# A hybrid decoder layer on one core: which weights are split by an accumulating transfer, and where the first casts and transposes stand

## The chip, the core and the metric

One core of a Trainium2 chip runs the whole layer as one program. TensorE (PE) multiplies, VectorE (DVE), ScalarE (ACT) and GpSimd (POOL) do elementwise work, SyncE (SP) issues transfers, and POOL issues some too. Each engine works through its own instructions in a fixed order. The metric is the device time of one execution in microseconds (us); less is better.

## The reference

One decoder layer in float32 with 1024 tokens of width 1024, cut to what matters here:

```
xn   = rms_norm(x, norm_mix)
proj = xn @ w_in          # [q | k/v for three branches | gates | conv in | q_mem | 3 merge gates]
...
a, ag = split(conv_in);  u = a * sigmoid(ag)      # then a causal convolution of 31 taps
...
qm = rms_norm(q_mem, mem_qk_norm[0])              # 4 heads of 128
km, vm = split(rms_norm(mem, norm_mem) @ w_mem_kv)
o_m = softmax(qm @ km.T) @ vm
...
merged = gm[0]*br_nsa + gm[1]*br_conv + gm[2]*br_mem
h = x + merged @ w_out
out = h + (silu(rms_norm(h) @ w_gate) * (rms_norm(h) @ w_up)) @ w_down
```

## The kernel before

Products are taken in float32r, a rounded form of float32 that TensorE runs in one pass. To keep the precision every operand is split in two tiles, high = rounded value and low = value - high, and a product is three matmuls: high x high, high x low, low x high (`mm3`, L151). For data the split (`split`, L130) is a cast on ACT and a subtraction on DVE. For most weights it is done otherwise (`unit`, L246, lines 254 to 257): ACT casts the loaded tile to the high half, ACT writes the negative of that into the low half, and a transfer that POOL issues adds the loaded tile to it in place. The loaded tile ("st", two buffers, or "fst", one buffer, for fill) can be loaded anew only when the transfer has landed; the split weights ("wsl") have three buffers, those for fill ("fsl") two.

The stages in the order of the program:

- Start: four pairs of row tiles of x (256 rows each). For each pair `norm_pair` (L200) takes two row sums of squares and roots on ACT, scales the rows on DVE (L207), transposes them on TensorE (16 transposes, L216) and splits the result into the eight tiles XN. `raw_proj` (L319) multiplies a pair with the first weights, the queries of the memory attention, heads 0 and 1 (48 products of 256 columns). The loop at L337 normalises and transposes pair tp + 1 ahead of the products of pair tp.
- The convolution's gate and input (L374 to L384, products of 512 columns), and from then on DVE's 124 taps (L371), laid along the products of the later stages.
- The branch gates, the inputs of the compressed keys and values (L410, whose sums are on POOL), their small network.
- The memory's norm and its keys and values (L480 to L492): eight weight tiles in four pairs.
- Memory attention for two pairs of heads (L552), which takes the next query products along; head norms (`head_norms`, L303).
- Convolution's layer norm, keys and values of two branches, attention, then the merge and the feed-forward part, which the change leaves alone.
- Fill (L781 to L794): the products for the merge gates, 24 weight tiles of 48 products of 512 columns, at the lowest priority. They go into the one PSUM bank named "pf"; after 24 products ACT copies it to "fz" (L793) and the bank is free again. Twelve of the tiles may run any time, the others are spread over the attention.

The order of each engine's instructions is fixed when the program is built, by a list scheduler that follows priorities (program order, with fill and taps put behind), its own estimate of durations, and order-only dependencies that the program adds by hand (`tc.add_manual_dep` with `ORDER`). At run time an instruction waits for its data and for the instruction before it on its engine.

Of the kernel before, what the change touches and what calls it, by code (L numbers as in the profile page):

```python
# [39 lines left out]
def hybrid_layer_kernel(  # L40
# [86 lines left out]
    def sub(eng, o, a, b):  # L127
        eng.tensor_tensor(o, a, b, op=OP.subtract)  # L128

    def split(hi, lo, src, eng=None):  # L130
        nc.scalar.copy(hi, src)  # L131
        sub(eng or nc.vector, lo, src, hi.bitcast(F32))

    def recip_rms(ss, n, eps, w):
        r = small(w)
        nc.scalar.activation(r, ss, AF.Sqrt, scale=1.0 / n, bias=eps)
        q = small(w)
        nc.vector.reciprocal(q, r)
        return q

    products = []

# [56 lines left out]

    def norm_pair(src, gain, dests, js):  # L200

        for tt in range(2):
            j = js[tt]
            ss = small(1)
            nc.scalar.activation(j, src[:, tt, :], AF.Square, accum_out=ss)
            r = recip_rms(ss, D, RMS_EPS, 1)
            nc.vector.scalar_tensor_tensor(j, src[:, tt, :], r, gain, op0=OP.mult, op1=OP.mult)  # L207
        transpose_pair(js, dests)

    def transpose_pair(js, dests):  # L210
        for kp in range(4):
            b = bank([2, 256])
            for kk in range(2):
                k = 2 * kp + kk
                for tt in range(2):
                    nc.tensor.transpose(b[:, kk, tt * P:(tt + 1) * P], js[tt][:, k * P:(k + 1) * P], ident)  # L216
            hi, lo = dests(kp)
            split(hi, lo, b)
# [16 lines left out]

    def norm_x(tp):
        half, q = tp // 2, tp % 2
        js = work2()
        if q == 0:
            for kp in range(4):  # L240
                XN[half][kp] = slab([2, 2, 512])
        norm_pair(xin[tp], gmix, lambda kp: tuple(XN[half][kp][:, hl, :, q * 256:(q + 1) * 256] for hl in range(2)),
                  js)


    def unit(src, shape, alloc=wslab, eng=None, load=False):  # L246
        if alloc is fslab:
            st = fstp.tile([P] + shape, F32, tag="fst", name=nm("fst"))
        else:
            st = stage.tile([P] + shape, F32, tag="st", name=nm("st"))  # L250
        ld = nc.sync.dma_start(st, src)
        w = alloc([2] + shape)
        hi, lo = w[:, 0], w[:, 1]
        if alloc is fslab or alloc is wslab:
            nc.scalar.copy(hi, st)
# [9 lines left out]

    def row_units(w, c0, alloc=wslab, eng=None):
        return [unit(w[u * 512:(u + 1) * 512, c0:c0 + 256].rearrange("(k p) c -> p k c", p=P), [4, 256], alloc, eng)
                for u in range(2)]

# [58 lines left out]
    for half in range(2):  # L328
        b = bank([512])
        nc.tensor.matmul(b, ones[0:1, :], g1[half], start=True, stop=True)  # L330
        nc.scalar.activation(gmix[:, half * 512:(half + 1) * 512], b, AF.Copy, scale=512.0)
    ws = row_units(w_in, C_QM)
    xin += [rows2(x, tp * 256) for tp in range(1, 4)]
    nc.sync.dma_start(gm, mem_qk_norm.to_broadcast([P, 2, P]))
    norm_x(0)
    QMQ = {}
    for tp in range(4):  # L337
        if tp < 3:
            norm_x(tp + 1)
        if tp == 0:  # L340
            QMQ[0] = slab([NT, 2, P], F32)
        raw_proj(ws, tp, QMQ[0])
# [31 lines left out]
    for ct in range(4):  # L374
        wag = col_unit(w_in, C_AG + ct * P)
        wa = col_unit(w_in, C_A + ct * P)
        uc = slab([2, S], F32)
# [32 lines left out]
    def compress_in(kind, c0):  # L410
        w = col_unit(w_in, c0, eng=nc.gpsimd)
        raw = t4([2, 512])
# [77 lines left out]
    for hp in range(2):  # L490
        ps = tok_proj(row_units(w_mem_kv, 512 + hp * 256, eng=nc.gpsimd), 0, mn)
        split(VM[:, 0, :, hp * 256:(hp + 1) * 256], VM[:, 1, :, hp * 256:(hp + 1) * 256], ps)  # L492
# [70 lines left out]

    QMQ[1] = slab([NT, 2, P], F32)
    mem_attention(0, row_units(w_in, C_QM + 256, eng=nc.gpsimd), QMQ[1])
    head_norms(QMQ[1], gm[:, 0, :])
    Q = [slab([NT, 4, 64], F32) for _ in range(2)]
    mem_attention(1, row_units(w_in, C_Q, eng=nc.gpsimd), Q[0])
    head_norms(Q[0], None)


    ws = row_units(w_in, C_Q + 256, eng=nc.gpsimd)
    for tp in range(4):
# [46 lines left out]
    for s, K, V in ((0, KS, VS), (1, KW, VW)):  # L620
        ws = row_units(w_in, C_KV + s * 256, eng=nc.gpsimd)

# [555 lines left out]
```

## Time and profile before

| | |
|---|---|
| median of the 3 runs shown | 1756.53 us (1756.08 to 1757.57) |
| the profiled execution | 1755.66 us, its span 1754.0 us |
| TensorE busy | 1710.8 us, 98% of the span |
| DVE, ACT, POOL busy | 58%, 45%, 33% |
| mean granted TensorE clock | 0.993 |
| accumulating transfers | 30 into "wsl", 24 into "fsl", 512 KB each |

In rows of the timeline the first number is the start, the second the time of the row's instructions together, then engine, line, operation, output <- input, sizes, and xN for N instructions; in brackets stands the idle time before them and what ended it. In rows of waits: the engine and its tile, what it waited for, microseconds in total, how often, the longest. A busy TensorE is not a TensorE at full rate, since the granted clock is lower for some time after idling.

### The profile page before, as it was taken

How to read it: one execution, taken by the hardware profiler on the slowest of the kernel's cores; microseconds unless marked ns; L12 is line 12 of the kernel's file. 1: busy time of each engine (PE TensorE's matmuls, PEld its weight loads, DVE VectorE, ACT ScalarE, POOL GpSimd, SP SyncE). 2: the span in 40 equal slices, each digit the busy share in tenths (PEclk: the TensorE clock that was granted, in tenths of full speed). 3: DMA queues.
4: the chain of work that ended last, by engine and by line, in shares of the span. 5: the costliest groups of instructions: out<-in, count | busy, mean ns of one | idle time of the engine just before them, and what ended most of it. 6: DMA issues, size and time to landing. Idle time of an engine off the chain costs nothing. (4 is left out here: it accounts for less than half of the span.)

```text
span 1754.0 us, 25341 instructions
## 1 busy us (share of the span) xinstructions
PE 1710.8 (98%) x9483; PEld 1488.0 (85%) x9483; DVE 1014.3 (58%) x1725; ACT 785.6 (45%) x1434; POOL 578.5 (33%) x549
## 2 busy tenths in 40 slices
PE   6899989999999999999999999999999999999999
PEld 5787879899988889999888899788888888888887
DVE  2488967635434556667754532865555454457655
ACT  5422554445366666767654422642222233233332
POOL 1100523224134434334303510156556767410000
PEclk9999999999999999999999999999999999999999
DMA  8344674544134222212286322233333445794673
GB/s 237 81 87 109 178 171 109 131 103 120 37 100 112 76 79 61 58 43 73 77 286 219 126 79 82 93 103 115 96 106 111 145 149 170 245 397 155 221 237 124
DMA packets 186165, 232.41 MB, mean 133 GB/s; under 512 B 11638, under 2 KB 126614, under 8 KB 185018
## 3 DMA queue, kind: packets, MB, share of 16 engines
q1 hardware_dynamic: 178266, 202.47, 34.8%
q0 software_dynamic: 7776, 28.32, 8.7%
q8 instruction: 75, 1.23, 0.3%
q14 instruction: 48, 0.39, 0.1%
HBM read 152.10 MB, written 50.33 MB: 115 GB/s over the span
## 5 line engine op out<-in xcount | busy, mean ns | idle before, releaser
L144 PE MATMUL ps<-slab,wsl 128*128 128x512 f32 (+1 forms) x1664 | 373.6, 383 | 6.1 <-POOL slab L423 3.1
L144 PEld LDWEIGHTS ps<-slab,wsl 128*128 128x128 f32 x1664 | 304.8, 190 | 67.2 <-POOL slab L423 3.3
L144 PE MATMUL pf<-slab,fsl 128*128 128x512 f32 x1236 | 322.4, 400 | 7.9 <-ACT fz L793 5.0
L144 PEld LDWEIGHTS pf<-slab,fsl 128*128 128x128 f32 x1236 | 224.4, 189 | 49.5 <-ACT fz L793 6.1
L144 PE MATMUL ps<-wsl,slab 128*128 128x256 f32 x1680 | 222.5, 289 | 6.7 <-DMA wsl<-st 5.7
L144 PEld LDWEIGHTS ps<-wsl,slab 128*128 128x128 f32 x1680 | 213.7, 197 | 10.1 <-DMA wsl<-st 6.6
L371 DVE SCALAR_TENSOR_TENSOR slab<-slab,cw 128x1021 f32<-128x1021 f32 (+15 forms) x120 | 163.1, 1362 | 2.4
L1008 DVE TENSOR_TENSOR t<-ps,t 128x512 f32<-128x512 f32 x127 | 86.9, 688 | 115.3 <-PE ps L144 114.1
L144 PE MATMUL ps<-slab,fsl 128*128 128x512 f32 x636 | 147.7, 389 | 0.0
L144 PEld LDWEIGHTS ps<-slab,fsl 128*128 128x128 f32 x636 | 119.4, 188 | 24.8
L128 DVE TENSOR_TENSOR t<-ps,t 128x512 fp32r<-128x512 f32 (+3 forms) x196 | 120.5, 632 | 31.5 <-ACT t L131 30.4
L1112 PE MATMUL ps<-wsl 128*128 128x512 f32 x495 | 118.5, 389 | 0.0
L144 PE MATMUL ps<-t,slab 128*128 128x256 f32 x624 | 116.3, 292 | 0.8 <-DVE t L128 0.8
L131 ACT CAST t<-ps 128x512 fp32r<-128x512 f32 (+2 forms) x192 | 98.9, 541 | 38.5 <-PE ps L742 26.6
L1112 PEld LDWEIGHTS ps<-wsl 128*128 128x128 f32 x495 | 92.9, 188 | 19.3
L144 PEld LDWEIGHTS ps<-t,slab 128*128 128x128 f32 x624 | 94.2, 190 | 6.6 <-DVE t L128 1.2
L144 PE MATMUL ps<-slab,qt 128*128 128x384 f32 (+3 forms) x384 | 95.1, 340 | 0.0
L656 POOL TENSOR_SCALAR wsl<-wsl,sm,gsb 128x640 f32<-128x640 f32 (+7 forms) x76 | 58.6, 781 | 93.1 <-DVE sm L651 86.6
L131 ACT CAST wsl<-t 128x1024 fp32r<-128x1024 f32 x42 | 44.3, 1054 | 98.3 <-POOL t L128 35.1
L257 POOL DMA_DIRECT2D wsl<-st x30 | 26.2, 883 | 182.4 <-ACT wsl L256 140.7
L1112 PE MATMUL ps<-fsl 128*128 128x512 f32 x330 | 79.8, 389 | 0.0
L1021 POOL TENSOR_TENSOR t<-t,t 128x512 f32<-128x512 f32 x21 | 39.2, 1865 | 116.7 <-DVE t L1008 43.8
(235 smaller groups left out, 2807.3 us busy)
## 6 DMA issues: line engine op xcount, KB each, us to landing
t<-in_w_down_dram SPq DMA_DIRECT2D x70, 256.0 KB, 4.3
wsl<-st POOLq DMA_DIRECT2D x30, 512.0 KB, 5.2
fst<-in_w_in_dram SPq DMA_DIRECT2D x24, 512.0 KB, 3.9
fsl<-fst POOLq DMA_DIRECT2D x24, 512.0 KB, 4.5
zd<-fz SPq DMA_DIRECT2D x48, 256.0 KB, 2.1
t<-zd SPq DMA_DIRECT2D x24, 512.0 KB, 3.9
st<-in_w_in_dram SPq DMA_DIRECT2D x22, 512.0 KB, 5.3
st<-in_w_gate_dram SPq DMA_DIRECT2D x22, 512.0 KB, 4.0
```

Source lines behind the costliest of these rows:

```text
L128: eng.tensor_tensor(o, a, b, op=OP.subtract)
L131: nc.scalar.copy(hi, src)
L144: m = nc.tensor.matmul(o, a, b, start=start, stop=stop)
L257: nc.gpsimd.dma_start(lo, st, accum_op=OP.add)
L371: return nc.vector.scalar_tensor_tensor(acc[:, s:], u[:, :S - s], cw[:, ct, 30 - s:31 - s], acc[:, s:], op0=OP.mult, op1=OP.add)
L656: nc.gpsimd.tensor_scalar(tiles[h], tiles[h], rec[:, h:h + 1], gsb[:, i, c0:c0 + 1], op0=OP.mult, op1=OP.mult)
L1008: nc.vector.tensor_tensor(o, a_, b_, op=OP.add)
L1021: nc.gpsimd.tensor_tensor(u4, u4, c22, op=OP.mult)
L1112: nc.tensor.matmul(B[t], a_, b_, start=start and k == 0 and j == 0, stop=k == FH - 1 and j == 2, skip_group_check=True)
```

## The change

`split` takes an engine as before, and with `nc.sync` it now does the negation and the accumulating transfer; without an engine DVE subtracts, with `nc.gpsimd` POOL does. `unit` no longer decides by the buffer, but by the engine that its caller names. The callers are set so: the convolution's weights, the compressed branches' inputs, the later query weights, the keys' and values' weights and fill from its fourth tile on keep the transfer (`eng=nc.sync`); the first weights and the eight tiles of the memory's keys and values go to DVE; the first three fill tiles go to POOL.

The casts of the first weights (`ready`) are taken out of the load and put, by an order-only dependency, behind the last root of pair 0 (`roots[-1]`). `norm_x` and the transposes (`turn_x`) are separate now: the transposes of pair 1 get an order-only dependency on the last product of pair 0, and those of the later pairs stand behind the products of the pair before in program order.

```
     def split(hi, lo, src, eng=None):
-        nc.scalar.copy(hi, src)
-        sub(eng or nc.vector, lo, src, hi.bitcast(F32))
+        first = nc.scalar.copy(hi, src)
+        if eng is nc.sync:
+            nc.scalar.activation(lo, hi.bitcast(F32), AF.Copy, scale=-1.0)
+            nc.gpsimd.dma_start(lo, src, accum_op=OP.add)
+        else:
+            sub(eng or nc.vector, lo, src, hi.bitcast(F32))
+        return first.ins
...
     def recip_rms(ss, n, eps, w):
         r = small(w)
-        nc.scalar.activation(r, ss, AF.Sqrt, scale=1.0 / n, bias=eps)
+        roots.append(nc.scalar.activation(r, ss, AF.Sqrt, scale=1.0 / n, bias=eps).ins)
...
-    def transpose_pair(js, dests):
+    def transpose_pair(js, dests, after=None):
...
-                    nc.tensor.transpose(b[:, kk, tt * P:(tt + 1) * P], js[tt][:, k * P:(k + 1) * P], ident)
+                    m = nc.tensor.transpose(b[:, kk, tt * P:(tt + 1) * P], js[tt][:, k * P:(k + 1) * P], ident)
+                    if after is not None:
+                        tc.add_manual_dep(m.ins, after.name, ORDER, reason="behind the products of the tiles before")
...
     def norm_x(tp):
+        js = work2()
+        norm_rows(xin[tp], gmix, js)
+        return js
+
+    def turn_x(tp, js, after=None):
         half, q = tp // 2, tp % 2
...
-        hi, lo = w[:, 0], w[:, 1]
-        if alloc is fslab or alloc is wslab:
-            nc.scalar.copy(hi, st)
-            nc.scalar.activation(lo, hi.bitcast(F32), AF.Copy, scale=-1.0)
-            nc.gpsimd.dma_start(lo, st, accum_op=OP.add)
+        if eng is None and ready is not None:
+            ready.append((w, st))
         else:
-            split(hi, lo, st, eng)
+            split(w[:, 0], w[:, 1], st, eng)
...
-    ws = row_units(w_in, C_QM)
+    ready = []
+    ws = row_units(w_in, C_QM, ready=ready)
...
-    norm_x(0)
-    QMQ = {}
+    turn_x(0, norm_x(0))
+    for w, st in ready:
+        tc.add_manual_dep(split(w[:, 0], w[:, 1], st), roots[-1].name, ORDER, reason="behind the first rows' sums")
+    js = norm_x(1)
+    QMQ = {0: slab([NT, 2, P], F32)}
     for tp in range(4):
-        if tp < 3:
-            norm_x(tp + 1)
-        if tp == 0:
-            QMQ[0] = slab([NT, 2, P], F32)
+        if tp:
+            turn_x(tp, js, products[-1][0] if tp == 1 else None)
+            js = norm_x(tp + 1) if tp < 3 else None
         raw_proj(ws, tp, QMQ[0])
...
-        wag = col_unit(w_in, C_AG + ct * P)
+        wag = col_unit(w_in, C_AG + ct * P, eng=nc.sync)
...
-        ps = tok_proj(row_units(w_mem_kv, hp * 256, eng=nc.gpsimd), 0, mn).rearrange("p t (h d) -> p t h d", h=2)
+        ps = tok_proj(row_units(w_mem_kv, hp * 256), 0, mn).rearrange("p t (h d) -> p t h d", h=2)
...
-            w = col_unit(w_in, C_GM + b_ * D + d_ * P, alloc=fslab, eng=nc.gpsimd)
+            w = col_unit(w_in, C_GM + b_ * D + d_ * P, alloc=fslab, eng=nc.sync if n_ > 2 else nc.gpsimd)
```

What this does to the order. On TensorE at the start, before, from the end of pair 0's transposes on (slab_175 holds pair 0's scaled rows, slab_222 pair 1's, slab_176 and slab_177 are tiles of XN, wsl_155 is the first weight tile):

```order
L216 MATMUL ps_215<-ident,slab_175 128x128 x3
L216 MATMUL ps_237<-ident,slab_222 128x128
L216 MATMUL ps_244<-ident,slab_222 128x128
L216 MATMUL ps_251<-ident,slab_222 128x128
L216 MATMUL ps_258<-ident,slab_222 128x128
L144 MATMUL ps_266<-wsl_155,slab_176 128x256
L216 MATMUL ps_237<-ident,slab_222 128x128 x3
L216 MATMUL ps_244<-ident,slab_222 128x128 x3
L216 MATMUL ps_251<-ident,slab_222 128x128 x3
L216 MATMUL ps_258<-ident,slab_222 128x128 x3
L144 MATMUL ps_266<-wsl_155,slab_176 128x256 x5
L144 MATMUL ps_266<-wsl_155,slab_177 128x256 x6
```

The same place now (slab_169 is pair 0, slab_220 pair 1, slab_184 to slab_187 tiles of XN, wsl_155 and wsl_158 the two weight tiles):

```order
L223 MATMUL ps_209<-ident,slab_169 128x128 x3
L149 MATMUL ps_236<-wsl_155,slab_184 128x256 x6
L149 MATMUL ps_236<-wsl_155,slab_185 128x256 x6
L149 MATMUL ps_236<-wsl_158,slab_186 128x256 x6
L149 MATMUL ps_236<-wsl_158,slab_187 128x256 x6
L149 MATMUL ps_236<-wsl_155,slab_184 128x256 x6
L149 MATMUL ps_236<-wsl_155,slab_185 128x256 x6
L149 MATMUL ps_236<-wsl_158,slab_186 128x256 x6
L149 MATMUL ps_236<-wsl_158,slab_187 128x256 x6
L223 MATMUL ps_286<-ident,slab_220 128x128
L223 MATMUL ps_293<-ident,slab_220 128x128
```

All 48 products of pair 0 stand ahead of pair 1's transposes now; before, one did. Further on, the second and third pair's products are no longer one block, and the first gate products of the convolution stand between pair 3's.

On ACT at the start, before, from the first row sum of pair 0 on (slab_143 is pair 0 as loaded, st_153 and st_159 are the loaded weights):

```order
L205 ACTIVATE slab_175,sm_180<-slab_143 128x1024
L136 ACTIVATE sm_182<-sm_180 128x1
L255 CAST wsl_155<-st_153 128x1024
L205 ACTIVATE slab_175,sm_187<-slab_143 128x1024
L256 ACTIVATE wsl_155<-wsl_155 128x1024
L255 CAST wsl_161<-st_159 128x1024
L136 ACTIVATE sm_189<-sm_187 128x1
L256 ACTIVATE wsl_161<-wsl_161 128x1024
L131 CAST slab_176<-ps_194 128x2x256
```

And now:

```order
L209 ACTIVATE slab_169,sm_170<-slab_143 128x1024
L141 ACTIVATE sm_172<-sm_170 128x1
L209 ACTIVATE slab_169,sm_177<-slab_143 128x1024
L141 ACTIVATE sm_179<-sm_177 128x1
L131 CAST wsl_155<-st_153 128x1024
L131 CAST wsl_158<-st_156 128x1024
L131 CAST slab_184<-ps_188 128x2x256
```

Both sums and roots of pair 0 stand ahead of the weights' casts, and the two negations are gone.

On DVE in the stage of the memory's keys and values, before (slab_850 is the third quarter of the convolution, the narrow numbers are its taps' lengths, t_188 the squares of the first pair's keys):

```order
L371 SCALAR_TENSOR_TENSOR slab_850<-slab_850,cw 128x1008
L293 TENSOR_REDUCE sm_1498<-t_188_1496 128x4
L128 TENSOR_TENSOR t_220_1736<-ps_1731,t_220_1736 128x512
L138 RECIPROCAL sm_1502<-sm_1500 128x4
L296 TENSOR_TENSOR t_187_1495<-ps_1446,sm_1502 128x512
L371 SCALAR_TENSOR_TENSOR slab_850<-slab_850,cw 128x1007
```

And now (wsl_1516, wsl_1588 and wsl_1593 are the weight tiles u3, u4 and u5 of eight):

```order
L383 SCALAR_TENSOR_TENSOR slab_848<-slab_848,cw 128x1008
L128 TENSOR_TENSOR wsl_1516<-st_1514,wsl_1516 128x1024
L302 TENSOR_REDUCE sm_1494<-t_188_1492 128x4
L383 SCALAR_TENSOR_TENSOR slab_848<-slab_848,cw 128x1007
L128 TENSOR_TENSOR wsl_1588<-st_1586,wsl_1588 128x1024
L128 TENSOR_TENSOR t_220_1726<-ps_1721,t_220_1726 128x512
L143 RECIPROCAL sm_1498<-sm_1496 128x4
L383 SCALAR_TENSOR_TENSOR slab_848<-slab_848,cw 128x1006
L305 TENSOR_TENSOR t_187_1491<-ps_1442,sm_1498 128x512
L383 SCALAR_TENSOR_TENSOR slab_848<-slab_848,cw 128x1005
L128 TENSOR_TENSOR wsl_1593<-st_1591,wsl_1593 128x1024
```

The weights' subtractions stand among the taps and the key norms. Later on TensorE, the order of fill among the other products is new too; until the first scores of the attention 408 fill products stand there now, before 360.

More of the change, by code (lines that the diff above doesn't have):

```diff
@@ L139, in recip_rms @@
         return q
-    products = []
+    products, roots = [], []
     def mm(o, a, b, start, stop):
@@ L198, in gain_row, with norm_rows @@
         return g
-    def norm_pair(src, gain, dests, js):
+    def norm_rows(src, gain, js):
         for tt in range(2):
@@ L207, in norm_pair @@
             nc.vector.scalar_tensor_tensor(j, src[:, tt, :], r, gain, op0=OP.mult, op1=OP.mult)
+    def norm_pair(src, gain, dests, js):
+        norm_rows(src, gain, js)
         transpose_pair(js, dests)
-    def transpose_pair(js, dests):
+    def transpose_pair(js, dests, after=None):
         for kp in range(4):
@@ L236, in norm_x @@
     def norm_x(tp):
+        js = work2()
+        norm_rows(xin[tp], gmix, js)
+        return js
+    def turn_x(tp, js, after=None):
         half, q = tp // 2, tp % 2
-        js = work2()
         if q == 0:
@@ L241, in norm_x, with unit @@
                 XN[half][kp] = slab([2, 2, 512])
-        norm_pair(xin[tp], gmix, lambda kp: tuple(XN[half][kp][:, hl, :, q * 256:(q + 1) * 256] for hl in range(2)),
-                  js)
-    def unit(src, shape, alloc=wslab, eng=None, load=False):
+        transpose_pair(js, lambda kp: tuple(XN[half][kp][:, hl, :, q * 256:(q + 1) * 256] for hl in range(2)), after)
+    def unit(src, shape, alloc=wslab, eng=None, load=False, ready=None):
         if alloc is fslab:
@@ L264, in col_unit, with row_units @@
                     load)
-    def row_units(w, c0, alloc=wslab, eng=None):
-        return [unit(w[u * 512:(u + 1) * 512, c0:c0 + 256].rearrange("(k p) c -> p k c", p=P), [4, 256], alloc, eng)
-                for u in range(2)]
+    def row_units(w, c0, alloc=wslab, eng=None, ready=None):
+        return [unit(w[u * 512:(u + 1) * 512, c0:c0 + 256].rearrange("(k p) c -> p k c", p=P), [4, 256], alloc, eng,
+                     ready=ready) for u in range(2)]
     def chan_proj(w, half, act=xn, n=P, alloc=bank):
@@ L374, in hybrid_layer_kernel @@
     for ct in range(4):
-        wag = col_unit(w_in, C_AG + ct * P)
-        wa = col_unit(w_in, C_A + ct * P)
+        wag = col_unit(w_in, C_AG + ct * P, eng=nc.sync)
+        wa = col_unit(w_in, C_A + ct * P, eng=nc.sync)
         uc = slab([2, S], F32)
@@ L410, in compress_in @@
     def compress_in(kind, c0):
-        w = col_unit(w_in, c0, eng=nc.gpsimd)
+        w = col_unit(w_in, c0, eng=nc.sync)
         raw = t4([2, 512])
@@ L490, in hybrid_layer_kernel @@
     for hp in range(2):
-        ps = tok_proj(row_units(w_mem_kv, 512 + hp * 256, eng=nc.gpsimd), 0, mn)
+        ps = tok_proj(row_units(w_mem_kv, 512 + hp * 256), 0, mn)
         split(VM[:, 0, :, hp * 256:(hp + 1) * 256], VM[:, 1, :, hp * 256:(hp + 1) * 256], ps)
@@ L564, in hybrid_layer_kernel @@
     QMQ[1] = slab([NT, 2, P], F32)
-    mem_attention(0, row_units(w_in, C_QM + 256, eng=nc.gpsimd), QMQ[1])
+    mem_attention(0, row_units(w_in, C_QM + 256, eng=nc.sync), QMQ[1])
     head_norms(QMQ[1], gm[:, 0, :])
     Q = [slab([NT, 4, 64], F32) for _ in range(2)]
-    mem_attention(1, row_units(w_in, C_Q, eng=nc.gpsimd), Q[0])
+    mem_attention(1, row_units(w_in, C_Q, eng=nc.sync), Q[0])
     head_norms(Q[0], None)
-    ws = row_units(w_in, C_Q + 256, eng=nc.gpsimd)
+    ws = row_units(w_in, C_Q + 256, eng=nc.sync)
     for tp in range(4):
@@ L620, in hybrid_layer_kernel @@
     for s, K, V in ((0, KS, VS), (1, KW, VW)):
-        ws = row_units(w_in, C_KV + s * 256, eng=nc.gpsimd)
+        ws = row_units(w_in, C_KV + s * 256, eng=nc.sync)
         def keys(tp, cat):
```

## The prediction

> **What bounds the kernel now.** I read the page's head first, then TensorE's waits, then stretches of the span, then the timeline of the stretches that lose time.
>
> ```profile
> span 1754.0 us, 25341 instructions
> PE 1710.8 (98%) x9483; PEld 1488.0 (85%) x9483; DVE 1014.3 (58%) x1725; ACT 785.6 (45%) x1434; POOL 578.5 (33%) x549
> ```
>
> TensorE (PE) is the bound: 43.2 us of 1754.0 are not busy. The change takes no matmul away, so it can win only idle time and slow matmuls. Who ends the idle time, longest first:
>
> ```profile
> PE ps L216 <- DVE slab L207: 10.6, 4, 3.6
> PE ps L144 <- DMA wsl<-st: 5.7, 4, 2.8
> PE pf L144 <- ACT fz L793: 5.0, 2, 4.3
> PE ps L216 <- DVE sm L138: 4.0, 1, 4.0
> PE ps L144 <- POOL slab L423: 3.1, 1, 3.1
> PE pf L144 <- ACT slab L131: 2.9, 1, 2.9
> ```
>
> And where it lies (columns: stretch, length, then busy time of PE, of the weight loads, DVE, ACT, POOL; PEclk is the granted clock):
>
> ```profile
> 9.60:67.50 57.90, 43.84 (x281) 40.75 (x282) 21.81 (x33) 30.34 (x55) 4.50 (x5) 0.94 0.62 159
> 192.90:217.00 24.10, 21.00 (x131) 19.24 (x132) 19.91 (x23) 17.60 (x33) 8.66 (x6) 0.93 0.61 141
> 217.00:283.00 66.00, 59.35 (x411) 55.50 (x410) 43.12 (x49) 32.88 (x54) 17.93 (x19) 0.95 0.79 189
> 321.00:334.00 13.00, 8.71 (x38) 7.17 (x38) 7.51 (x9) 6.66 (x10) 7.13 (x5) 0.87 0.25 79
> ```
>
> Four stretches hold 28.1 of the 43.2 us: the start (14.1), a wait for POOL (3.1), the memory keys and values (6.7), the head norms (4.3). The change's moved instructions stand in the first, third and fourth.
>
> **The start.** T0 to T3 are the transposes of the four pairs of row tiles (16 each), P0 to P3 their products with the first weights (48 each). TensorE's timeline, with "..." for rows left out:
>
> ```profile
> 13.54 2.82 PE L216 MATMUL ps<-ident,slab 128*128 128x128 f32 x12 [2.85 <-DVE slab L207]
> ...
> 23.71 2.23 PE L144 MATMUL ps<-wsl,slab 128*128 128x256 f32 x12
> 28.82 0.79 PE L144 MATMUL pf<-slab,fsl 128*128 128x512 f32 x1 [2.88 <-ACT slab L131]
> 29.41 11.17 PE L144 MATMUL ps<-wsl,slab 128*128 128x256 f32 x83
> 40.41 5.40 PE L144 MATMUL pf<-slab,fsl 128*128 128x512 f32 x23
> ...
> 47.22 1.53 PE L216 MATMUL ps<-ident,slab 128*128 128x128 f32 x12 [0.73 <-DVE slab L207]
> 52.80 1.09 PE L216 MATMUL ps<-ident,slab 128*128 128x128 f32 x4 [4.05 <-DVE sm L138]
> ...
> 58.31 9.23 PE L144 MATMUL ps<-wsl,slab 128*128 128x256 f32 x75
> ```
>
> P3 ends at 58.31 + 9.23 = 67.5. A transpose costs 1.53 / 12 = 0.13 us here and 2.82 / 12 = 0.24 after a wait; a 256-column product 9.23 / 75 = 0.12, and 2.23 / 12 = 0.19 after one; a 512-column product 5.40 / 23 = 0.23. The bulk of P0 and P1 starts only at 29.41, because P0's second weight tile is cast late, negated, and then added to by a transfer. The other engines in the same time:
>
> ```profile
> 7.74 0.20 ACT L136 ACTIVATE sm<-sm 128x1 f32<-128x1 f32 x1
> ...
> 8.84 1.05 ACT L205 ACTIVATE slab<-slab 128x1024 f32<-128x1024 f32 x1
> ...
> 12.20 1.28 DVE L207 SCALAR_TENSOR_TENSOR slab<-slab,sm,t 128x1024 f32<-128x1024 f32 x1
> ...
> 14.48 2.51 ACT L131 CAST slab<-ps 128x512 fp32r<-128x512 f32 x4 [1.53 <-PE ps L216]
> 15.10 2.61 DVE L128 TENSOR_TENSOR slab<-ps,slab 128x512 fp32r<-128x512 f32 x4 [1.61 <-ACT slab L131]
> ...
> 18.17 1.04 ACT L205 ACTIVATE slab<-slab 128x1024 f32<-128x1024 f32 x1
> ...
> 19.89 1.28 DVE L207 SCALAR_TENSOR_TENSOR slab<-slab,sm,t 128x1024 f32<-128x1024 f32 x1
> ...
> 26.16 1.04 ACT L255 CAST fsl<-fst 128x1024 fp32r<-128x1024 f32 x1 [6.62 <-DMA fst<-in_w_in_dram]
> ...
> 39.61 1.05 ACT L255 CAST fsl<-fst 128x1024 fp32r<-128x1024 f32 x1 [7.34 <-DMA fst<-in_w_in_dram]
> ```
>
> The second row sum (8.84) now follows the first root (7.74 + 0.20 = 7.94), no weight cast between. Undisturbed, a row sum starts 1.72 us ahead of its scaling (18.17 to 19.89), so the second scaling runs from 9.7 to 10.9, not to 13.5, and T0 ends at 10.9 + 2.8 = 13.8. That the second row has landed by 7.94 no row shows; by 8.84 it had, so at worst 0.9 is lost. ACT casts both weights (1.04 each) from about 9.3, under the scaling; DVE subtracts them right behind it. The price of such a subtraction is 1.23 us (row L128 below), so to 13.4; T0's four differences (2.61 / 4 = 0.65 each) wait behind these, and the first is there at 14.1. That is P0's start, with both weight tiles complete.
>
> From there I add up TensorE. P0: 48 products, 5.8 us at 0.12, 8.9 at 0.19; I take 6.7, about a dozen of them slow, since TensorE has by then worked for 3 us: to 20.8. T1 stands behind P0, 16 x 0.13 = 2.0, to 22.9; its scalings lie under P0. Behind P0, ACT first copies its result, sums a row of pair 2 (1.05) and squares half a row (copy and square are half as wide, taken as 0.6 each), and only then casts T1: a first difference at about 24.6, so TensorE waits 1.7 us. P1 with two fill products and short waits for its later casts then ends at about 31.5. Next, in the new order: four of T2, 19 fill, 12 of T2, 3 fill: 0.5 + 4.4 + 1.5 + 0.7, to 38.6. P2 5.8, to 44.4; T3 2.0, to 46.4; a wait of 0.7 for its first cast and difference; P3 5.8 with one fill and 17 products of the convolution's gate between (18 x 0.23 = 4.1): 57.0. P3 ends 10.5 us earlier with 18 products (4.1 us) done that stood behind it: **a gain of 14.6; I take 14.** The work of ACT and DVE stays hidden only if loads come in time: the fill weight's cast (26.16) now stands among T1's casts, the second's (39.61) ahead of T2's. At their old times they would hold TensorE 2 and 3 us longer; I expect them earlier, since two accumulating transfers no longer share the queues and the fill weight's staging tile comes free after a POOL subtraction. With the row 0.9 late and P0 slow (2.2), the gain is 6; all products fast and no waits, 16.5.
>
> **Memory keys and values.** Eight weight tiles (u0 to u7, a pair per 48 products), before by an accumulating transfer, now by a DVE subtraction. TensorE and one cast, then the prices of a transfer, a DVE and a POOL pass:
>
> ```profile
> 222.12 1.05 ACT L255 CAST wsl<-st 128x1024 fp32r<-128x1024 f32 x1 [5.30 <-PE ps L144]
> 253.59 1.04 ACT L255 CAST wsl<-st 128x1024 fp32r<-128x1024 f32 x1 [4.43 <-DMA st<-in_w_in_dram]
> ```
>
> ```profile
> 229.28 5.95 PE L144 MATMUL ps<-wsl,slab 128*128 128x256 f32 x35 [2.83 <-DMA wsl<-st]
> ...
> 255.99 5.95 PE L144 MATMUL ps<-wsl,slab 128*128 128x256 f32 x35 [0.91 <-DMA wsl<-st]
> ...
> 273.79 9.22 PE L144 MATMUL ps<-wsl,slab 128*128 128x256 f32 x74
> ```
>
> ```profile
> wsl<-st POOLq DMA_DIRECT2D x30, 512.0 KB, 5.2
> ```
>
> ```profile
> L128 DVE TENSOR_TENSOR wsl<-st,wsl x35: 1211/1225/2331, 880.2 to 1727.5; 128x1024 fp32r<-128x1024 f32 x35
> ```
>
> ```profile
> L591 POOL TENSOR_TENSOR slab<-slab,slab x6: 2400/2570/3325, 187.0 to 412.6; 128x1024 f32<-128x1024 f32 x6
> ```
>
> The loss there is 6.65 us idle plus twice 35 products at 0.17 for 0.12 (1.7 each): 10 us. From the cast of u3 (222.12) to its first use (229.28) go 7.2 us. Now it is 1.05 + at most one convolution tap of DVE ahead (its pass is as long as a 1024-wide scaling, 1.28) + 1.23 = 3.6 us, ready at about 225.7 on the old clock; TensorE finishes what stands ahead, seven more fill products among it, at about the same time. The later pairs gain more, since a staging tile comes free 4 us sooner and the next load can start. What is left: the next weights (u8, u9) still go through the transfer, and u9's load starts when u7 is subtracted. In the new order only 24 products of u8 and a few others stand ahead of u9's low half, where before 26 fill products covered it (up to 273.79). I count that at 3 us lost: **a gain of 7**, between 2 (u9 late by a full landing of 5.2 and slow products after it) and 10 (nothing lost).
>
> The Trainium skill ("DMA: Bandwidth & Descriptors", section "Anatomy of one DMA — SWDGE (gpsimd) path") puts a POOL-issued transfer at 2.0 us plus bytes over 436 GB/s: an estimate of 3.2 us for 512 KB. The rows say 5.2. By that rule a subtraction would save 2 us less per tile and this term would be about 4 for 7; the trace has the duration for this transfer, so I keep 7.
>
> DVE takes 8 x 1.23 = 9.8 us more. It idles 66.0 - 43.1 = 22.9 us in this stretch, so the taps keep up. ACT loses a negating pass (1.05) for each of the thirteen tiles that leave the transfers, POOL an issue; both had room. SP's row of loads is the same up to the memory weights. The three fill tiles that POOL now subtracts (2.4 to 3.3 us) take the place of a landing of 5: nothing.
>
> **Head norms.** What holds TensorE there:
>
> ```profile
> 315.42 5.63 PE L144 MATMUL pf<-slab,fsl 128*128 128x512 f32 x24
> ...
> 322.14 1.15 ACT L309 ACTIVATE t<-slab 128x512 f32<-128x512 f32 x2 [5.84 <-DMA md<-t]
> ...
> 325.34 6.22 PE L144 MATMUL pf<-slab,fsl 128*128 128x512 f32 x19 [4.29 <-ACT fz L793]
> ```
>
> ACT waits for a transfer out, and the copy that frees the only fill bank stands behind that. The chain is untouched. In the new order 5 fill products, not 24, stand between the last memory product and that bank change (4.4 us less cover), but the copy moves ahead of a table load and a root, and the transfer out no longer queues right behind a load. I take **1.5 us lost**, between 1 gained and 4 lost. The POOL wait of 3.1 stays: its chain of taps and POOL sums keeps its order and shifts as a whole.
>
> **The sum.** -14 - 7 + 1.5 = -19.5. The profiled execution took 1755.66 (span 1754.0 and 1.66 around it): 1736.2. The median of the runs shown, 1756.53, is 0.9 above it, so I predict 1737.
>
> **Rivals.**
> Only the start gains: u8 and u9, or DVE's row of taps, eat the second term: -14 + 1.5, 1744. For it: the transfers stay for those two tiles and less fill covers them. Against: 22.9 us of idle DVE.
> Late loads: the first 30 us are full of transfers, and the fill weights come when they came before; start 6, the second term 4: 1748. For it: the casts at 26.16 and 39.61 both waited for their loads. Against: two 512 KB transfers fewer.
> The waits only move, for instance into the head norms, whose stall grows by as much: within 3 us of 1756.5. Against: TensorE's order at the start is dense whatever comes later.
> Slower: DVE works in order, and a subtraction whose tile is not cast yet holds the taps, the softmax maxima and the norms behind it, and TensorE needs the last two. If each of the eight waited as the cast at 253.59 did (4.43), DVE would stand 35 us in place of the 10 lost now: +25 - 14 + 1.5 = +13, 1769. It costs something once the waits pass the idle time left, (22.9 - 9.8) / 8 = 1.6 us per tile, and the sign turns where they cost TensorE 10 + 12.5, 2.8 us per tile. Against: loads now start sooner.
>
> **How the numbers follow.** Forecast 0.62; only the start 0.18; late loads 0.10; moved waits 0.05; slower 0.05. A measurement of this kernel can tell about 0.2%, 3.5 us, from no change: the first three cases are faster (0.90), the fourth the same (0.05), the fifth slower (0.05). The forecast's ends are 16.5 + 10 + 1 = 27.5 gained (1729) and 6 + 2 - 4 = 4 (1753); both rarely come together. With the second and third case inside, 8 in 10 lie in 1730 to 1748.
>
> **What would show it.** Right: the 256-column products run from about 14 us on with no wait over 2 us before 57 us; P3 ends near 57; no wait of TensorE for a transfer into a weight tile between 200 and 240. Wrong: P0 starting after 18 us, ACT waiting for fill loads ahead of T1's or T2's casts, DVE idle with the cast of a weight as releaser, or attention and what follows (from about 480 us, 1274 us now) longer than now.

## The result and the profile after

| | before | after |
|---|---|---|
| median | 1757.05 us (1756.08 to 1757.61, 4 runs) | 1729.64 us (1728.72 to 1730.32, 4 runs) |
| ratio to before | | 0.9844, interval 0.9827 to 0.9861 |
| profiled execution, its span | 1755.66, 1754.0 us | 1730.32, 1727.7 us |

The change makes the kernel 27.4 us faster. The prediction said 1737, 8 in 10 between 1730 and 1748: the right direction, and 0.36 us outside the range, on the fast side (two of the four executions, 1730.01 and 1730.32, lie inside). The head of the page after, and its software queue (POOL's accumulating transfers: packets, MB, share; before 7776 packets and 28.32 MB, so the 6.8 MB of the thirteen tiles are gone):

```profile
PE 1702.5 (99%) x9483; PEld 1480.3 (86%) x9483; DVE 1024.3 (59%) x1735; ACT 772.2 (45%) x1421; POOL 574.2 (33%) x539
...
q0 software_dynamic: 5904, 21.50, 6.7%
```

TensorE is idle for 1727.7 - 1702.5 = 25.2 us, 43.2 before. Of its waits, the row of 5.7 us for a transfer into a weight tile is gone, and of the 10.6 + 4.0 us for the scaled rows one wait of 3.6 is left, the first of all, and 0.2; the waits for POOL and for the fill bank stay:

```profile
PE pf L149 <- ACT fz L805: 4.2, 2, 3.8
PE ps L149 <- POOL slab L435: 3.2, 1, 3.2
PE ps L223 <- DVE sm L143: 3.6, 1, 3.6
```

**The start.** TensorE's timeline after. P0 is the row at 13.35, P1 stands between 23.18 and 30.1, P2 is the row at 36.89, P3 ends with the row at 50.16:

```profile
10.88 2.82 PE L223 MATMUL ps<-ident,slab 128*128 128x128 f32 x12 [0.22 <-DVE slab L211]
13.35 7.12 PE L149 MATMUL ps<-wsl,slab 128*128 128x256 f32 x48
20.31 1.91 PE L223 MATMUL ps<-ident,slab 128*128 128x128 f32 x16
23.18 0.50 PE L149 MATMUL ps<-wsl,slab 128*128 128x256 f32 x2 [0.97 <-ACT slab L131]
...
36.89 5.91 PE L149 MATMUL ps<-wsl,slab 128*128 128x256 f32 x48
...
46.28 4.04 PE L149 MATMUL ps<-slab,wsl 128*128 128x512 f32 x17
50.16 4.96 PE L149 MATMUL ps<-wsl,slab 128*128 128x256 f32 x40
54.96 5.40 PE L149 MATMUL ps<-slab,wsl 128*128 128x512 f32 x23
```

After the first row no idle time is longer than 0.97 us. What follows P3 starts at 54.96, before at 67.38:

```profile
67.38 4.95 PE L144 MATMUL ps<-slab,wsl 128*128 128x512 f32 x21
```

That is 12.4 us earlier, with 17 gate products (4.04 us) already done: **16.5 us gained**. The loads were in time for TensorE. ACT after, at the two fill casts that the prediction feared:

```profile
23.50 1.07 ACT L131 CAST fsl<-fst 128x1024 fp32r<-128x1024 f32 x1
...
30.73 1.05 ACT L131 CAST fsl<-fst 128x1024 fp32r<-128x1024 f32 x1 [2.07 <-DMA fst<-in_w_in_dram]
```

The first has no wait, where 26.16 had 6.62; the second still waits 2.07 us for its load, but comes 9 us earlier and delays nothing of TensorE's.

**The POOL wait.** First before, then after:

```profile
196.00 3.49 PE L144 MATMUL ps<-slab,wsl 128*128 128x128 f32 x16 [3.11 <-POOL slab L423]
```

```profile
181.43 2.05 PE L149 MATMUL ps<-slab,wsl 128*128 128x128 f32 x16 [3.23 <-POOL slab L435]
```

The wait is the same, but the 16 products behind it took 2.05 us, not 3.49: 1.3 gained in sum. The granted clock over them was 0.54 before and 1.00 after. That this comes from the change is not shown: in four of the runs below that keep nearly all of the change (memory weights by transfer, transposes ahead, all fill by transfer, two query tiles on DVE) the same wait was followed by 3.04 to 3.78 us for the same 16 products.

**Memory keys and values.** From the first product with w2s, the second weights of the small network (200.48 before, 184.48 after), to the end of the last memory product, before and after (columns: stretch, length, busy time of the fill products ("pf") alone, granted clock, share of DMA, GB/s):

```profile
200.48:315.58 115.10, 35.80 (x141) 0.97 0.64 147
```

```profile
184.48:293.09 108.61, 38.09 (x152) 1.00 0.48 124
```

Without fill the stretch takes 115.10 - 35.80 = 79.3 us before and 108.61 - 38.09 = 70.5 after: **8.8 gained**. The prediction feared the tenth tile, u9. POOL issued its transfer at 239.68 and it landed 4.5 us later, at 244.2, just as the block of 70 products that needs it begins; the block runs at full rate, with no idle time ahead:

```profile
239.68 0.87 POOL L134 DMA_DIRECT2D wsl<-st  x1 [6.64 <-DVE sm L528]
```

```profile
244.27 8.63 PE L149 MATMUL ps<-wsl,slab 128*128 128x256 f32 x70
```

**Head norms, and all behind them.** TensorE after; then ACT's wait for the transfer out and its copy that frees the fill bank, after; then TensorE and that copy before:

```profile
292.94 1.33 PE L149 MATMUL pf<-slab,fsl 128*128 128x512 f32 x5
298.03 7.38 PE L149 MATMUL pf<-slab,fsl 128*128 128x512 f32 x24 [3.77 <-ACT fz L805]
305.24 1.04 PE L513 MATMUL ps<-ident,slab 128*128 128x128 f32 x8
```

```profile
295.32 2.19 ACT L318 ACTIVATE t<-slab 128x512 f32<-128x512 f32 x4 [7.85 <-DMA md<-t]
...
297.42 0.56 ACT L805 COPY fz<-pf 128x512 f32<-128x512 f32 x1
```

```profile
324.72 0.57 ACT L793 COPY fz<-pf 128x512 f32<-128x512 f32 x1
...
331.40 0.60 PE L501 MATMUL ps<-ident,slab 128*128 128x128 f32 x4
```

From 292.94 to 305.24 go 12.30 us with 1.33 + 7.38 of fill: 3.6 lost; before, from 315.42 to 331.40, 15.98 with 5.63 + 6.22: 4.1 lost. So 0.5 gained. The cover shrank from 24 to 5 products, 4.3 us (5.63 - 1.33), but the copy now comes 4.5 us (292.94 to 297.42) after the last memory product, and before 9.3 (315.42 to 324.72). Most of that is the transfer out: it released ACT at 295.32, 2.4 us after 292.94, and before at 322.14, 6.7 us after 315.42. Everything behind takes as long as before (columns as in the prediction):

```profile
331.40:1754.00 1422.60, 1413.32 (x7798) 1229.73 (x7796) 791.92 (x1490) 643.06 (x1192) 501.75 (x472) 1.00 0.41 130
```

```profile
305.24:1727.70 1422.46, 1413.16 (x7793) 1229.26 (x7791) 791.76 (x1492) 642.69 (x1192) 502.32 (x472) 1.00 0.41 130
```

All is won in the first 331 us: 331.40 - 305.24 = 26.2. Added up: 16.5 + 1.3 + 8.8 + 0.5 = 27.1. The 0.9 between is about the size of the five more fill products that are done by then (five matmuls fewer in that last row, 1.2 us at 0.23). The part behind could be shorter by as much, but is shorter by 0.14 only; where that went is not shown.

### The profile page after: what moved, and what is told of

Read it like the earlier page. It is cut to its first block, busy times and chain, and to the rows that moved or that the text cites. A ratio compares the mean times of both kernels' runs of the same rounds, so it can differ in the third digit from the quotient of the medians.

```text
span 1727.7 us, 25318 instructions
## 1 busy us (share of the span) xinstructions
PE 1702.5 (99%) x9483; PEld 1480.3 (86%) x9483; DVE 1024.3 (59%) x1735; ACT 772.2 (45%) x1421; POOL 574.2 (33%) x539
## 3 DMA queue, kind: packets, MB, share of 16 engines
q8 instruction: 74, 1.21, 0.3%
## 5 line engine op out<-in xcount | busy, mean ns | idle before, releaser
L149 PE MATMUL ps<-wsl,slab 128*128 128x256 f32 x1680 | 217.2, 285 | 1.5 <-ACT slab L131 1.0
L149 PEld LDWEIGHTS ps<-wsl,slab 128*128 128x128 f32 x1680 | 208.9, 193 | 4.5 <-ACT slab L131 1.5
L383 DVE SCALAR_TENSOR_TENSOR slab<-slab,cw 128x1021 f32<-128x1021 f32 (+16 forms) x120 | 164.7, 1377 | 2.1
L131 ACT CAST wsl<-st 128x1024 fp32r<-128x1024 f32 x65 | 68.2, 1051 | 99.2 <-PE ps L149 49.2
L128 DVE TENSOR_TENSOR wsl<-st,wsl 128x1024 fp32r<-128x1024 f32 x45 | 60.2, 1339 | 36.0 <-ACT wsl L131 32.7
```

The costliest lines, as they stand in the source:

```text
L131: first = nc.scalar.copy(hi, src)
L149: m = nc.tensor.matmul(o, a, b, start=start, stop=stop)
L383: return nc.vector.scalar_tensor_tensor(acc[:, s:], u[:, :S - s], cw[:, ct, 30 - s:31 - s], acc[:, s:], op0=OP.mult, op1=OP.add)
```

## The experiments

Each run is one edit of the kernel after or of the kernel before. Times are medians of 4 executions, 10 for the first row of the memory weights on DVE; the kernel before, run beside them, had medians of 1756.69 to 1757.39 us. The rows shown are of one execution each; for the memory weights by transfer (1740.13 us) and the transposes (1735.27) that execution was 2.0 and 3.0 us above the median.

| experiment | base | median us | ratio to before, interval |
|---|---|---|---|
| memory weights by transfer | after | 1738.10 | 0.9897, 0.9883 to 0.9912 |
| first weights by transfer | after | 1744.95 | 0.9934, 0.9919 to 0.9949 |
| first casts in the old place | after | 1733.73 | 0.9871, 0.9856 to 0.9886 |
| transposes ahead of products | after | 1732.25 | 0.9861, 0.9845 to 0.9878 |
| memory weights on DVE alone | before | 1753.11 | 0.9977, 0.9967 to 0.9986 |
| the same, negation first | before | 1748.61 | 0.9950, 0.9936 to 0.9965 |
| the same, ten tiles on DVE | before | 1748.83 | 0.9952, 0.9937 to 0.9967 |
| all fill by transfer | after | 1733.37 | 0.9862, 0.9845 to 0.9878 |
| no transfers but for fill | after | 1733.39 | 0.9865, 0.9850 to 0.9879 |
| two query tiles on DVE | after | 1728.30 | 0.9835, 0.9820 to 0.9849 |
| wide sum on DVE | after | 1729.77 | 0.9843, 0.9828 to 0.9857 |
| four tiles more on DVE | after | 1732.42 | 0.9859, 0.9844 to 0.9873 |

**Memory weights by transfer** (the other part of the change is left).

```
-        ps = tok_proj(row_units(w_mem_kv, 512 + hp * 256), 0, mn)
+        ps = tok_proj(row_units(w_mem_kv, 512 + hp * 256, eng=nc.sync), 0, mn)
```

These are the values; the keys have the same edit. 

> The changed kernel (1729.6 us) with one part undone: the eight weight tiles of the memory's keys and values go through the accumulating transfer again. Theory A (the landing time of these transfers held TensorE, and DVE's subtraction removed that, 9 us between the end of the gates' stage and the last memory product): 1738 to 1740, and TensorE waits for transfers into weight tiles come back, 5 us or more in all. Rival B (the start's gain is nearly all, and the new order of fill would cover the landings as well): 1730 to 1732.

Measured 1738.10, 8.5 us more than after, as theory A said. The waits for transfers into weight tiles are back, and so are the slow products behind them; TensorE's waits, then one of them in its timeline:

```profile
PE ps L149 <- DMA wsl<-st: 6.5, 4, 2.8
```

```profile
213.08 7.13 PE L149 MATMUL ps<-wsl,slab 128*128 128x256 f32 x35 [2.79 <-DMA wsl<-st]
```

**First weights by transfer.**

```
-        tc.add_manual_dep(split(w[:, 0], w[:, 1], st), roots[-1].name, ORDER, reason="behind the first rows' sums")
+        tc.add_manual_dep(split(w[:, 0], w[:, 1], st, nc.sync), roots[-1].name, ORDER, reason="behind the first rows' sums")
```

> The changed kernel with the first two weight tiles split by negation and accumulating transfer again, still behind the second row sum. Theory A (pair 0's products started at 13.4 us because no transfer stood between cast and use): they start at 19 to 22 us, 1735 to 1738. Rival B (the order of casts and transposes alone made the start; the transfer is hidden): 1730 to 1732.

Measured 1744.95, 15.3 us more than after and well above theory A's figure: nearly the whole gain of the start. TensorE waits twice, and the second wait has its cause on ACT:

```profile
20.99 8.29 PE L149 MATMUL ps<-wsl,slab 128*128 128x256 f32 x47 [7.13 <-DMA wsl<-st]
...
36.16 0.79 PE L149 MATMUL ps<-wsl,slab 128*128 128x256 f32 x2 [5.14 <-ACT slab L131]
```

```profile
25.77 1.05 ACT L131 CAST fsl<-fst 128x1024 fp32r<-128x1024 f32 x1 [8.33 <-DMA fst<-in_w_in_dram]
...
33.06 1.04 ACT L131 CAST fsl<-fst 128x1024 fp32r<-128x1024 f32 x1 [3.33 <-DMA fst<-in_w_in_dram]
```

The casts of T1 (at 35.53 and 36.53) stand behind fill casts that wait for loads. The first of these loads was issued at 11.94 and its cast could run at 25.77, 13.8 us later; after, it was issued at 12.42 and had landed by 23.50 at the latest, 11.1 us. So this is the rival "late loads": it comes with the two transfers, and without them it does not. That sharing the queues is what slows the load is argued, not shown.

**First casts in the old place**: `ws = row_units(w_in, C_QM)`, so the casts are free to stand between the two row sums, as before; they still end in DVE subtractions. 

> The changed kernel without the order-only dependency of the first weight casts on the second root: the casts stand where the scheduler puts them, ahead of the second row sum if it does as before. Theory A: the second scaling ends 1 to 2.5 us later, and so do the transposes of pair 0 and all behind them: 1731 to 1732.5. Rival B (the casts' place is worth nothing, TensorE is held by the subtractions anyway): 1729 to 1730.

Measured 1733.73, 4.1 more than after, above theory A's range. The second scaling is late again, and T0 with it:

```profile
13.74 2.82 PE L223 MATMUL ps<-ident,slab 128*128 128x128 f32 x12 [2.88 <-DVE slab L211]
...
54.11 4.96 PE L149 MATMUL ps<-wsl,slab 128*128 128x256 f32 x40
```

P3's last row starts 4.0 us later than after (54.11 for 50.16). T0 accounts for 2.9 of these (13.74 for 10.88). Behind it fill stands in another order among P1's products, and the granted clock there was 0.86 (25.86 to 37.94), where after it was 1.00 (23.18 to 36.89); the rest is not split further.

**Transposes ahead of products.**

```
-        if tp:
-            turn_x(tp, js, products[-1][0] if tp == 1 else None)
-            js = norm_x(tp + 1) if tp < 3 else None
+        if tp < 3:
+            turn_x(tp + 1, js)
+            js = norm_x(tp + 2) if tp < 2 else None
```

> The changed kernel with each pair's transposes ahead of the pair before's products again, as in the kernel before, everything else new. Theory A (three causes share the start's 16 us; this one is 4 to 6 of them, since TensorE in its fixed order waits at pair 1's transposes for a scaling that ends near 18.5 us while pair 0's products could run): 1733 to 1736. Rival B (this order makes nearly the whole start): 1742 or more. Rival C (once the weights are there in time, the order is worth nothing): 1729 to 1731.

Measured 1732.25, 2.6 more than after, a little under theory A's range. T1's first row sits in front of P0 and waits for its scaling:

```profile
17.15 1.12 PE L223 MATMUL ps<-ident,slab 128*128 128x128 f32 x4 [3.47 <-DVE slab L211]
```

So each of the three edits of the start adds something, and they are unequal: the first weights' subtractions are worth 15.3 us on top of the other two, the place of the casts 4.1, the order of the transposes 2.6. For the last two the intervals of the ratios overlap a little with that of the kernel after; the executions themselves do not (1732.01 and more, against 1730.32 and less). Together the three make 22.0, more than the 16.5 of the start, so they are not shares of it.

**Memory weights on DVE alone**, in the kernel before.

```
-        if alloc is fslab or alloc is wslab:
+        if (alloc is fslab or alloc is wslab) and eng is not nc.vector:
...
-        ps = tok_proj(row_units(w_mem_kv, 512 + hp * 256, eng=nc.gpsimd), 0, mn)
+        ps = tok_proj(row_units(w_mem_kv, 512 + hp * 256, eng=nc.vector), 0, mn)
```

> The kernel before, with one part of the change alone: the eight weight tiles of the memory's keys and values are subtracted by DVE, everything else (start, fill, other weights) as before. Theory A (each part gains its own idle time and slow products, 9.0 us for this one by the milestones of the two traces): 1747 to 1749, TensorE's wait of 5.7 us for a transfer into a weight tile gone. Rival 1 (the prediction's term of 7 with 3 us still lost at the ninth and tenth tile): 1750 to 1752, with a wait of TensorE for a transfer near 260 to 275 us. Rival 2 (the gain came with the new fill order of the start, 19 fill products more done by then): 1754 or more.

Measured 1753.11: only 3.7 us gained. That lies between rival 1 (1750 to 1752) and rival 2 (1754 or more). The trace has the sign of rival 1, a wait for a transfer near 260 to 275 us. Here the prediction's fear comes true, u9 is late: the block of 70 products waits and then runs at 10.16 / 70 = 0.145 us each, not 0.123. The cause is ACT's row: u9's cast, the next tile's cast, which waits for its load, and only then the two negations.

```profile
265.65 10.16 PE L144 MATMUL ps<-wsl,slab 128*128 128x256 f32 x70 [3.61 <-DMA wsl<-st]
```

```profile
254.57 1.05 ACT L255 CAST wsl<-st 128x1024 fp32r<-128x1024 f32 x1
...
258.54 1.05 ACT L255 CAST wsl<-st 128x1024 fp32r<-128x1024 f32 x1 [2.43 <-DMA st<-in_w_in_dram]
...
259.49 2.00 ACT L256 ACTIVATE wsl<-wsl 128x1024 fp32r<-128x1024 f32 x2
```

In the kernel after, the negation (at 238.21) stands ahead of the next cast (241.37). Whether this is the whole difference the next run tests.

**The same, negation first**: one order-only dependency more. The list `negs` holds the negations; only the next query weights, the eleventh and twelfth tile, come with `nc.sync`, and the eleventh's cast is the one that this moves.

```
-            nc.scalar.copy(hi, st)
+            cast = nc.scalar.copy(hi, st)
+            if eng is nc.sync:
+                tc.add_manual_dep(cast.ins, negs[-1].name, ORDER, reason="behind the negation before")
```

> The kernel before with the memory's eight weight tiles on DVE, and one order-only dependency more: the cast of the eleventh weight tile stands behind the negation of the tenth on ACT, as it does by itself in the kernel after (in the kernel with that part alone the cast stood ahead, waited 2.43 us for its load, and TensorE then waited 3.61 us for the tenth tile). Theory A (that order on ACT is what ate about half of the part's 9 us there, 3.6 us idle and 70 products at 0.145 for 0.12 us, 1.6): 1747 to 1749.5, no wait of TensorE for a transfer into a weight tile over 1 us. Rival (the tenth tile is late anyway, by its load and its landing): 1752 to 1754, a wait of 2 us or more stays.

Measured 1748.61, 4.5 us faster than without the dependency (the intervals of the ratios do not touch). u9's negation now follows its cast at once, and the block runs without a wait at 0.124 us each:

```profile
256.02 1.05 ACT L257 CAST wsl<-st 128x1024 fp32r<-128x1024 f32 x1
...
257.46 1.06 ACT L260 ACTIVATE wsl<-wsl 128x1024 fp32r<-128x1024 f32 x1
...
259.93 1.05 ACT L257 CAST wsl<-st 128x1024 fp32r<-128x1024 f32 x1 [1.41 <-DMA st<-in_w_in_dram]
```

```profile
263.54 8.66 PE L144 MATMUL ps<-wsl,slab 128*128 128x256 f32 x70
```

**The same, ten tiles on DVE**: u8 and u9 (`C_QM + 256`) with `eng=nc.vector` as well. 

> The kernel before with ten weight tiles on DVE: the memory's eight and the ninth and tenth, the query weights behind them. Theory A (the tenth tile alone held the part back in the kernel before; by DVE it has neither a negation nor a landing): 1746.5 to 1749. Rival 1 (what the start's change gives is needed for the rest of the 9 us, the fill and the loads being further ahead): 1751 to 1754.

Measured 1748.83, the same as the run before: it is u9 in time that counts, by either way. So the memory part alone, with that order on ACT, is worth 1757.39 - 1748.61 = 8.8 us on the old start, and 8.5 on the new one. What is left without it, 1738.10, is 18.6 below the 1756.69 run beside it. The two parts add up to the whole: 8.8 + 18.6 = 27.4. The 18.6 hold the start, the fill tiles on POOL and all else.

**All fill by transfer**: `eng=nc.sync` for every fill tile. 

> The kernel after, with the first three fill tiles by the accumulating transfer as before, in place of a subtraction on POOL. Theory A (the prediction's: they take the place of a landing of 5 us, nothing gained or lost): 1729 to 1731. Rival (without them the loads of the first 30 us come late, since the fill tile's buffer is free later and a transfer shares the queues): ACT stands at the second fill cast ahead of pair 2's casts as with the first weights by transfer, 1733 to 1740.

Measured 1733.37. That is 3.7 us more than after by the medians; the intervals of the ratios overlap by a little, but the trace shows 3.2 us of it, since P3's last row starts at 53.35 for 50.16. TensorE waits for the first fill weight, and ACT for the second fill tile's load (in the kernel after this load was issued at 27.09 and its cast ran at 30.73, here 31.93 and 36.82):

```profile
31.91 4.87 PE L149 MATMUL pf<-slab,fsl 128*128 128x512 f32 x20 [1.93 <-DMA fsl<-fst]
```

```profile
36.82 1.05 ACT L131 CAST fsl<-fst 128x1024 fp32r<-128x1024 f32 x1 [5.99 <-DMA fst<-in_w_in_dram]
```

**No transfers but for fill**: every other `eng=nc.sync` taken out, so DVE subtracts all of those weights. 

> The kernel after, with every weight that still goes through an accumulating transfer subtracted by DVE in its place, but for the fill tiles from the fourth on: convolution, compressed branches, later queries, keys and values of the branches. Theory A (these weights have time to spare, so the shorter split gains nothing, and DVE, nearly full with taps from 100 to 200 us, gets some 25 us more work and is late for the sums that POOL and TensorE wait for): 1732 to 1740, the wait near 181 us longer than 3.2 us. Rival (DVE has room everywhere and a subtraction is never worse than a transfer): 1727 to 1730.

Measured 1733.39, 3.8 more than after (the intervals of the ratios overlap by a little), as theory A said, but not by its sign: the wait near 181 us is gone (on POOL the compressed branches' sums now stand ahead of a sum of the convolution). The time is lost some 15 us later, at the small network and the memory's rows:

```profile
PE ps L149 <- ACT t L453: 4.9, 1, 4.9
PE ps L223 <- DVE slab L211: 4.4, 3, 3.7
```

**Two query tiles on DVE**: u8 and u9 without `eng=nc.sync`. 

> The kernel after, with two weight tiles more on DVE: the ninth and tenth of the row, the query weights for the first memory attention, which still go through the transfer. Theory A (they land in time, TensorE does not wait there, nothing is left to gain): 1729 to 1731, as the kernel after. Rival (the prediction's 3 us at the tenth tile are lost in a way that the waits do not show, for instance as slow products): 1726 to 1727.5. Second rival (the subtractions hold the softmax maxima behind them on DVE): 1732 or more.

Measured 1728.30. The median is 1.3 us under the kernel after and the intervals of the ratios overlap for the most part: the runs do not tell the two apart, and nothing says that 3 us were lost at u9.

**Wide sum on DVE**: `nc.vector` for the sum of L435. 

> The kernel after, with the wide sum in the inputs of the compressed branches (two instructions of 128 x 1024) on DVE, not POOL; TensorE's order is word for word that of the kernel after. Theory A (TensorE's 3.2 us near 181 us are POOL's row of taps' sums and these sums): the wait shrinks to under 1 us, 1726 to 1727.5. Rival 1 (the wait only moves to what is next late, a fill bank or the small network's casts): 1729 to 1730. Rival 2 (DVE is full there, and the sum queued behind taps comes later than on POOL): 1731 or more.

Measured 1729.77, nothing gained. The sum on DVE stands behind a row of taps and ends at 180.54 (177.53 + 3.01), on POOL at 181.38 (177.98 + 3.40); TensorE still waits:

```profile
169.53 8.09 DVE L383 SCALAR_TENSOR_TENSOR slab<-slab,cw 128x995 f32<-128x995 f32 x5
177.53 3.01 DVE L435 TENSOR_TENSOR slab<-t,pos 128x1024 f32<-128x1024 f32 x1
```

```profile
180.65 2.02 PE L149 MATMUL ps<-slab,wsl 128*128 128x128 f32 x16 [2.44 <-issue]
```

**Four tiles more on DVE**: the compressed branches' inputs and u8, u9 without `eng=nc.sync`. 

> The kernel after, with four weight tiles more on DVE: the compressed branches' two inputs and the ninth and tenth tile. On POOL the sums of both compressed branches then stand ahead of a sum of the convolution, by the order of the instructions. Theory A (TensorE's 3.2 us near 181 us come from that sum of 3.3 us ahead of them on POOL, and it does not come back): 1724.5 to 1727, the wait under 1 us. Rival (POOL's sum of the convolution is now late for DVE's taps, or the small network waits for casts, as in the kernel without transfers, where 4.9 and 4.4 us came back near 195 us): 1728 to 1731.

Measured 1732.42, 2.8 more than after (the intervals of the ratios overlap). The POOL wait is gone, and a longer one takes its place, for the memory's scaled rows, which DVE makes between its taps:

```profile
193.80 0.69 PE L223 MATMUL ps<-ident,slab 128*128 128x128 f32 x2 [5.22 <-DVE slab L211]
```

In three runs (no transfers, wide sum, four tiles more) the wait near 181 us was taken away or shortened, and each time nothing was won; in two of them the traces show what is late next, work that stands in DVE's row. Of the twelve none beats the kernel after by more than the runs can tell.

## Why the prediction missed

The mechanisms were mostly right. What failed is the size of the terms, all in one direction: the start 2.5 us too small, the memory 1.8, the head norms 2.0 and the POOL wait 1.3, which makes 27.1 in the traces for 19.5 in the sum. At u9, and with the three fill tiles, the reasoning was wrong too.

- **Start, 14 predicted, 16.5 measured, the end that was called good.** P0 started at 13.35 (14.1 predicted), P1's waits were 1.0 and 0.3 (1.7 and "short waits"), T3's wait of 0.7 did not come, and P3 ended at 55.1, not 57.0. A further 0.6 had been rounded off, from a sum of 14.6. P0 with a dozen slow products was taken as 6.7 and measured 7.1. So the good end's condition, all products fast and no waits, was not met, and that its number came out is luck; by the prediction's own terms (P0 at 0.12 and no wait of 1.7 and 0.7) that end should have been 14.6 + 0.9 + 1.7 + 0.7 = 17.9. Both fears (a late second row, late loads) did not come true. The rival "late loads" was a real mechanism: it is what the first weights' transfers bring about.
- **A reading of the start before.** The prediction says that P0 and P1 start in bulk only at 29.41 because P0's second weight tile is late. Its transfer was issued at 13.26 and landed 10.2 us later, at 23.5. TensorE's 2.88 us ahead of 28.82 end with ACT's cast of T1, and that stood behind the fill cast at 26.16, which had waited 6.62 us for its load. So by these rows it was the load that held the bulk until 29.41, as it held T1's casts in the run with the first weights by transfer (5.14 us).
- **Three fill tiles on POOL, "nothing" predicted.** Wrong: 3.2 us of the start hang on them (inside the 16.5, not on top), 1.9 as a wait for the landing itself, and the rest, by the rows, because the one fill staging tile is free 5 us later for the next load, which ACT then waits for ahead of T2's casts. The prediction named this staging tile among the reasons for earlier loads, and priced it at nothing two paragraphs later.
- **Memory keys and values, 7 predicted, 8.8 measured** (8.5 and 8.8 by two undone runs). The step that failed: "I count that at 3 us lost" at u9. It measured zero in the kernel after. The reason it gave, too few products ahead of u9's low half, was not the one that decided on the old start: with memory weights alone u9 was late by 3.6 us and its products slow, and the order of two instructions on ACT removed both. DVE's row of taps kept up, as said; the slower rival found no support. Two of the prediction's signs of being wrong did show, both small and without cost to TensorE: ACT's 2.07 us for a fill load ahead of T2's casts, and DVE idle for the casts of the memory weights, 2.1 us in all.
- **The two prices of a transfer.** By the estimate of 3.2 us from the Trainium skill ("DMA: Bandwidth & Descriptors", section "Anatomy of one DMA — SWDGE (gpsimd) path") the term was 4. By the row's 5.2 it was 7. Both carry the 3 us at u9 that were not lost; without them they are 7 and 10, on either side of the 8.8 measured. So the total decides little between the two; the transfers' own rows decide it, 5.2 us before (30 of them) and 4.8 after (20).
- **Head norms, 1.5 lost predicted, 0.5 gained measured.** Both mechanisms of that step were there: cover shorter by 4.3 us, copy earlier by 4.8. The earlier copy was taken as 2.9 us (4.4 less cover for 1.5 lost), and that was the size that was off; it is the transfer out that came 4.3 us earlier behind the last memory product (2.4 us for 6.7).
- **The POOL wait "stays"**: it stayed, 3.23 us. That the products behind it would be faster by 1.4 us was not foreseen, and is not shown to be the change's doing.
- **The range.** The ends' own sum was 27.5 gained, and the step "both rarely come together" cut the good end to 1730. It failed because the middle values were not middles: each had a loss taken off for a wait that the new order might bring (the waits in P1 and T3, 3 us at u9, 1.5 at the head norms). Of these only P1's came, 1.3 us in all, so the terms came out near the good end together. The 1.3 us of the faster products are more than the 0.36 by which the range was missed.

## What to carry to other kernels

A split weight that the bound engine needs early was better finished by an engine than by a transfer here (15.3 us for the first weights, 8.5 for the memory's). Where it had time to spare, moving it bought nothing that the runs can tell and may cost something, since it lengthens the row of the engine that takes it over (1733.39 for 1729.64 with all but the fill on DVE). Before counting a landing as late, read the order on the engine whose work stands ahead of it: a cast that waits for the next load, ahead of a negation whose inputs are ready, cost 4.5 us here. And when a forecast takes off a loss for each wait that might appear, price the case in which none of them does, and keep it in the range.

## What the runs showed of the hardware

The same wait was not always followed by slow products. Behind the 3.1 to 3.2 us for POOL the 16 products took 3.49 us before at a granted clock of 0.54, 2.05 after at 1.00, and 2.05 to 3.78 in the other runs that have this wait. These are the same 16 products of 128 columns each time; what decides it these runs do not show. So a lower clock behind an idle time of this length is not certain, and a difference of 1 to 2 us between two traces can come from it alone.

One DVE pass beside a two-input pass of POOL took almost three times as long as alone. After, a tap at 195.84 took 3.41 us where its neighbour took 1.27, while POOL subtracted a fill tile (3.49 us from 194.70, where the subtractions at 24.65 and 31.87 took 2.41 and 2.39). DVE's own subtraction, begun together with POOL's at 194.72, took its usual 1.21, so running beside POOL was not enough to slow a pass. The sums look as if the passes took turns: 1.21 + 2.4 = 3.6 is close to POOL's 3.49, and the tap ended 1.1 us after POOL's pass, close to its own 1.27. It is one such place, and no run tests it:

```profile
193.33 1.27 DVE L383 SCALAR_TENSOR_TENSOR slab<-slab,cw 128x1013 f32<-128x1013 f32 x1
...
194.72 1.21 DVE L128 TENSOR_TENSOR wsl<-st,wsl 128x1024 fp32r<-128x1024 f32 x1
195.84 3.41 DVE L383 SCALAR_TENSOR_TENSOR slab<-slab,cw 128x1012 f32<-128x1012 f32 x1
```

```profile
194.70 3.49 POOL L128 TENSOR_TENSOR fsl<-fst,fsl 128x1024 fp32r<-128x1024 f32 x1 [11.08 <-ACT fsl L131]
```
